# Three gate tiles in place of two behind attention, squares of the attention's result on two engines, LayerNorm begun in the gate tiles

## The chip, the cores and the metric

The kernel runs on one core of a Trainium2 chip. The metric is the device time of one execution in microseconds; the median of three executions of the kernel before is 1280.73 us (1280.35 to 1281.03). A profile is one execution of its own, and its time stands beside the median below. The engines are named as the profile names them: PE multiplies matrices (PEld loads its weights), ACT is ScalarE, DVE is VectorE, POOL is GpSimd, SP issues the DMA transfers.

## The reference

One layer of a streaming encoder: 1024 frames of a new stream and 32 frames of a running one with 512 frames behind it, width 1024, 16 heads of 64. In the reference's terms, with all 1056 frames written as one x:

```
h  = rmsnorm(x)
q, k, v, logf, ga, ua, ub, gb, ma, mb = columns of h @ w_in          # each 1024 wide, logf 16
u  = ua * sigmoid(ub);   conv = causal depthwise conv of u, width 31
o  = softmax(q k' + C[t] - C[s]) v,  C = cumsum(log f), causal, q and k rms-normed per head
ya = (o * silu(ga)) @ w_pa
yb = (silu(layernorm(conv)) * silu(gb)) @ w_pb
m  = sigmoid(ma) * ya + sigmoid(mb) * yb
y  = x + m @ w_out
```

Keys, values, forget gates and the last rows of u are outputs too.

## The kernel before

**Tiles.** Everything is computed transposed: channels on the 128 partitions, the 1056 frames along the free axis. A projection makes 128 output channels at a time, from 8 tiles of input channels ("kt") and 3 chunks of 352 frames. Each number is a sum of two fp16 halves, so that one product is three matmuls: high weight by high input, low by high, high by low (line 199). Three matmuls of one kt and one chunk are a *beat*; an output tile has 24 beats.

**Weights.** Two tiles of weights (512 KB each) are prepared together, as a `Batch`. SP loads them (L111, L180); ACT squares each with the sum along a row (L119, output `junk`, a buffer that nothing reads); POOL casts the two sums (L125); PE totals them over the partitions with a matmul (L132, tile `tot`); DVE makes from that a power of two for the scale (L173, L174, tile `sc`); ACT makes the high halves (L154, `wh`) and DVE the low ones in three pieces (L157, `wl`). The scale of a pair serves both tiles. The batch of the *next* pair is prepared beside the matmuls of this one: the squares 3 and 13 beats after the first tile of the pair begins, the total at its 25th beat, the high halves 29 and 39 beats behind the start, the low ones behind those.

**Order.** PE, ACT, DVE and SP run a written order: `later(n, fn)` puts a piece of work n beats behind the present one, `beat()` issues what has become due, and each engine takes its instructions in the order so issued. An engine that waits holds up all that stands behind it. POOL's order is left to a scheduler. In the last stage (the output projection) SP is free too.

**Stages.** Input projections, convolution, q, k and v, the gate ga (to about 600 us); attention (about 600 to 987 us); a stretch between attention and projections (to about 1012 us) with what is left of the gate tiles; the projection pa (`outproj("pa")`, 192 beats) with LayerNorm beside it; the projection pb; the output projection.

**Attention** runs over 128 units: 8 pairs of heads, 8 blocks of 128 queries, 2 heads. A unit has its products of queries and keys (L1259 to 1261, `psS`), the maximum (DVE, L1268), the exponentials on ACT (L1274, L1289), then the high and low halves PH, transposed by DMA (L1306, tile PT), then, per group of four units and LAG = 8 units later, the products with the values (L1327, `po`). The 24 tiles of the gates gb, ma and mb (`fills`) are the filler: NFILL of them are issued in beats between the units, as many per unit as the number `each` allows, and 36 beats of them behind the last unit, around the last groups of value matmuls. The result goes to DRAM (`s_o`, L1344).

**Between attention and projections.** NFILL = 22, so two gate tiles are left (`last_gate`, 48 beats). Beside them run:

- `a_load`: eight loads of the attention's result, 512 KB each, into tiles `wide` (L1555), at tick 0
- `a_square`: a copy of the 32 sample columns by DVE (L1558) and the square with its row sum on ACT (L1537), at ticks 5 + 3f; the squares' own output goes to `ah`, to be overwritten later
- `norm_a.total` at tick 30: PE's `ptot` (L1542), then DVE's scale `nsc` (L1543, L173, L174)
- `norm_a.halves` at ticks 31 + 2f: high half `ah` on ACT (L1548), low half `al` on DVE (L1549)

**LayerNorm**, per tile f of 128 channels, at 16 beats from one tile to the next: `ln_load` (the convolution's result and the gate gb), `ln_centre` (DVE, L1571 and L1572, from the mean and rstd computed earlier), `ln_swish` (ACT, a Silu of each, L1576 and L1577), `ln_gate` (DVE, L1581), `ln_square` (ACT, L1537). Tile f is centred 2 + 16f beats behind the start of pa. When all are squared, `norm_c.total` (a second `ptot`) and `norm_c.halves` (`c_h`, `c_l`) follow, and then pb can begin.

pa's tiles are evacuated by DVE (L1672) with the gate ma, through a Tanh on ACT (L1639, tile `sma`), which wants another table than the Silu. For each change of table ACT loads one (`ACT_TABLE_LOAD`).

Of the kernel before, what the change touches and what calls it, by code (L numbers as in the profile page):

```python
# [10 lines left out]
BF16 = mybir.dt.bfloat16  # L11
F16 = mybir.dt.float16
I32 = mybir.dt.int32
AF = mybir.ActivationFunctionType
ALU = mybir.AluOpType
# [5 lines left out]
TT = T + TS  # L21
# [3 lines left out]
KT = 8  # L25
# [6 lines left out]
LNEXP = "natural_log_exp_and_others"  # L32
NFILL = 22
R_U, R_V, R_QK, R_G, R_A = 0.21, 0.18, 0.165, 0.23, 0.7
# [23 lines left out]
def build(tc, xT, xt, wv, wf, ckT, cv, clT, stT, vec, cst, yT, kT, vO, lfO, cpT, csT):  # L58
# [33 lines left out]
    class Batch:  # L92


        def __init__(self, keys):
            self.keys = keys
            self.n = len(keys)
            self.raws = []
# [110 lines left out]
    def later(n, fn):  # L209

        pace["n"] += 1
        late.append((pace["tick"] + n, pace["n"], fn))
        late.sort(key=lambda e: e[:2])
# [1204 lines left out]
    K = range(len(units))  # L1418
    each = (BEAT * (24 * NFILL - 36) + sum(map(matmuls, K))) / sum(map(heavy, K))
    events = {}  # L1420
# [101 lines left out]
    class Norm:  # L1522


        def __init__(self, g, junk):
            self.g, self.junk, self.x = g, junk, {}
            self.n8 = cp.tile([128, 8], F32, name="n8", tag="n8", bufs=2)
            self.sc = cp.tile([128, 4], F32, name="nsc", tag="nsc", bufs=2)
            self.back = self.sc[:, 3:4]
            sides["back_" + g] = self.back  # L1530
# [4 lines left out]

        def square(self, f):
            nc.scalar.activation(self.junk()[:, f, :].bitcast(BF16), self.x[f], AF.Square, accum_out=self.n8[:, f:f + 1])  # L1537

# [12 lines left out]

    norm_a = Norm("pa", lambda: ah)

# [3 lines left out]
    def a_square(f):  # L1557
        nc.vector.tensor_copy(norm_a.x[f][:, T:], os_t[:, f, :])  # L1558
        norm_a.square(f)

# [18 lines left out]
    def ln_gate(f):  # L1579
        y = norm_c.x[f]  # L1580
        nc.vector.tensor_mul(y, y, lng.pop(f))  # L1581

    def ln_square(f):
        if not chl:
            chl.extend(cpl.tile([128, KT, TT], F16, name=a, tag=a) for a in ("c_h", "c_l"))
        norm_c.square(f)

# [3 lines left out]

    norm_c = Norm("pb", lambda: chl[0])
    n_gate = 24 * len(fills)
    n_pa, n_pb = n_gate, n_gate + 192
    for f in range(8):
        a_load(f)
        later(5 + 3 * f, lambda f=f: a_square(f))
        later(31 + 2 * f, lambda f=f: norm_a.halves(f, ah, al))
        t = n_pa + 16 * f
        for n, fn in ((-16, ln_load), (2, ln_centre), (8, ln_swish), (13, ln_gate), (16, ln_square)):  # L1600
            later(t + n, lambda f=f, fn=fn: fn(f))
        later(n_pa + 136 + 5 * f, lambda f=f: norm_c.halves(f, *chl))
        t = n_pa + 24 * f
        later(t - 18, lambda f=f: pa_load(f))
        later(t + 1, lambda f=f: pa_gate(f))
        t = n_pb + 24 * f
        later(t - 12, lambda f=PBO[f]: pb_load(f))
        later(t + 1, lambda f=PBO[f]: pb_gate(f))
    later(30, norm_a.total)
    later(n_pa + 134, norm_c.total)  # L1610
    for j in range(3):
# [8 lines left out]
    w_next = []  # L1620
    later(n_pb + 150, lambda: w_next.append(load_raw(("out", 0))))
    later(n_pb + 176, lambda: w_next.append(split_w(w_next.pop(0))))
    sma, ya, mixed = {}, {}, {}

# [21 lines left out]
    cpl = pool("cpl", 1, stack=pcl)  # L1646
    yap = pool("yap", 2, stack=pcl)

    def outproj(g, rh, rl, mk, order=range(8)):
# [83 lines left out]
    order = ExitStack()  # L1733
    order.enter_context(tc.manual_schedule(engines={E.PE, E.DVE, E.Activation}))

# [105 lines left out]
    firsts = [w_next.pop()]  # L1841
    raws = [load_raw(("out", 2))]
    both = [big("r0")]
# [117 lines left out]
```

## Time and profile before

| | before |
|---|---|
| median of three executions | 1280.73 us |
| the profiled execution | 1278.86 us |
| its span | 1277.1 us |
| granted TensorE clock, mean over the span | 0.988 |
| PE busy | 1230.6 us, 96% |
| DVE busy | 1022.4 us, 80% |
| ACT busy | 779.2 us, 61% |
| POOL busy | 556.0 us, 44% |
| tick 0 of the stretch between (its first gate matmul behind the last value matmul) | about 987 us |
| PE's first wait for a total of squares | 1005.20 us |

The span is what the profiler recorded of the program on the engines; the execution's time has a little around it. Idle time of an engine counts only where the engine that ends last waits for it. In the rows that follow, a line number is one of the kernel before; "out<-in" are the names of the tiles; a number in square brackets is the wait ahead of the instruction, with the engine, the tile and the line that ended it.

### The profile page before, as it was taken

How to read it: one execution, taken by the hardware profiler on the slowest of the kernel's cores; microseconds unless marked ns; L12 is line 12 of the kernel's file. 1: busy time of each engine (PE TensorE's matmuls, PEld its weight loads, DVE VectorE, ACT ScalarE, POOL GpSimd, SP SyncE). 2: the span in 40 equal slices, each digit the busy share in tenths (PEclk: the TensorE clock that was granted, in tenths of full speed). 3: DMA queues.
4: the chain of work that ended last, by engine and by line, in shares of the span. 5: the costliest groups of instructions: out<-in, count | busy, mean ns of one | idle time of the engine just before them, and what ended most of it. 6: DMA issues, size and time to landing. Idle time of an engine off the chain costs nothing.

```text
span 1277.1 us, 24881 instructions
## 1 busy us (share of the span) xinstructions
PE 1230.6 (96%) x9288; PEld 856.9 (67%) x9288; DVE 1022.4 (80%) x1453; ACT 779.2 (61%) x1480; POOL 556.0 (44%) x541
## 2 busy tenths in 40 slices
PE   8999999999999999999898998989989899999998
PEld 5677786666666666666665565666657556666898
DVE  5799898888988989798998998976873477577764
ACT  5645655768677684456776666667764878444410
POOL 4058483728566561013554655534442000122662
PEclk8999999999999999999999999999989999999999
DMA  6335251433324247445999999999987876543561
GB/s 233 102 109 148 60 146 43 114 91 111 115 78 123 73 133 224 132 133 154 208 212 227 209 211 214 212 209 213 222 191 185 303 270 206 203 152 119 158 184 63
DMA packets 259802, 207.38 MB, mean 162 GB/s; under 512 B 186464, under 2 KB 222176, under 8 KB 259680
## 3 DMA queue, kind: packets, MB, share of 16 engines
q1 hardware_dynamic: 259536, 205.71, 60.2%
q8 instruction: 73, 1.20, 0.4%
q14 instruction: 49, 0.40, 0.1%
q10 hardware_dynamic: 144, 0.07, 0.0%
HBM read 110.84 MB, written 57.12 MB: 132 GB/s over the span
## 4 chain that ended last, share of the span: by engine, by line
PE 72%; DVE 10%; ACT 5%; issue 5%; DMA 4%; POOL 3%; SPq 0%; DVEq 0%; POOLq 0%; ACTq 0%
PE pj L199 50%; PE pjv L830 7%; PE pj L1791 6%; PE po L1327 2%; DMA PT<-PH 2%; PE psS L1259 2%; PE psS L1260 2%; DVE y L392 1%; DVE nm L1268 1%; POOL PH L1296 1%; DVE wl L157 1%; DVE PH L1298 1%; POOL P L1295 1%; DMA wide<-s_o 1%; ACT PH L1289 1%
## 5 line engine op out<-in xcount | busy, mean ns | idle before, releaser
L199 PEld LDWEIGHTS <-wh 128*128 128x128 f16 x3840 | 377.5, 98 | 207.2 <-issue 6.2
L199 PE MATMUL pj<-xh,wh 128*128 128x352 f16 (+2 forms) x1536 | 482.9, 314 | 0.6 <-DVE qn L976 0.5
L199 PE MATMUL pj<-xl,wh 128*128 128x352 f16 (+2 forms) x1536 | 482.0, 314 | 1.3 <-DVE xl L614 1.3
L199 PE MATMUL pj<-xh,wl 128*128 128x352 f16 (+2 forms) x1536 | 482.2, 314 | 0.1
L392 DVE SCALAR_TENSOR_TENSOR y<-u,vec_t,y 128x1086 f32<-128x1086 f32 x240 | 354.2, 1477 | 4.0 <-ACT y L389 0.9
L199 PEld LDWEIGHTS <-wl 128*128 128x128 f16 x1920 | 188.6, 98 | 89.6 <-issue 1.0
L157 DVE SCALAR_TENSOR_TENSOR wl<-raw,sc,wh 128x384 f16<-128x384 f32 (+1 forms) x236 | 170.1, 743 | 40.8 <-ACT wh L154 39.9
L1274 ACT ACTIVATE P<-psS,nm 128x1024 f32<-128x1024 f32 (+7 forms) x128 | 94.4, 738 | 99.6 <-DVE nm L1268 38.9
L1295 POOL TENSOR_SCALAR P<-P,nm 128x896 f32<-128x896 f32 (+3 forms) x64 | 63.8, 996 | 190.3 <-ACT PH L1289 184.4
L1268 DVE TENSOR_REDUCE nm<-psS 128x1 f32<-128x1024 f32 (+7 forms) x128 | 96.2, 752 | 47.6 <-PE psS L1261 32.4
L1289 ACT ACTIVATE PH<-P,nm 128x1024 f16<-128x1024 f32 (+7 forms) x128 | 98.6, 770 | 9.7 <-DMA PT<-PH 7.7
L1296 POOL TENSOR_TENSOR PH<-P,PH 128x896 f16<-128x896 f32 (+3 forms) x64 | 95.1, 1486 | 5.0
L119 ACT ACTIVATE junk<-raw 128x1024 bf16<-128x1024 f32 x78 | 81.7, 1048 | 5.2 <-DMA raw<-wf 5.1
L961 POOL TENSOR_TENSOR sql<-sqf,sqh 128x352 fp32r<-128x352 f32 x48 | 55.8, 1165 | 65.0 <-ACT sqh L958 64.8
L1259 PE MATMUL psS<-KB,QB 128*128 128x512 f16 (+2 forms) x192 | 64.4, 336 | 19.4 <-ACT P L1274 19.1
L125 POOL CAST topb<-tops 128x2 bf16<-128x2 f32 x32 | 14.8, 462 | 151.8 <-ACT junk L119 151.6
L1298 DVE SCALAR_TENSOR_TENSOR PH<-P,nm,PH 128x896 f16<-128x896 f32 (+3 forms) x64 | 61.7, 964 | 12.7 <-ACT PH L1289 11.5
L154 ACT ACTIVATE wh<-raw,sc 128x1024 f16<-128x1024 f32 (+1 forms) x58 | 64.9, 1124 | 11.0 <-DVE sc L174 11.0
L830 PE MATMUL pjv<-vwh,xh 128*128 128x260 f16 x256 | 70.1, 274 | 0.0
L830 PE MATMUL pjv<-vwl,xh 128*128 128x260 f16 x256 | 70.0, 273 | 0.0
L830 PE MATMUL pjv<-vwh,xl 128*128 128x260 f16 x256 | 69.9, 273 | 0.0
L987 POOL TENSOR_TENSOR ql<-qn,qh 128x352 f16<-128x352 f32 (+1 forms) x48 | 65.7, 1385 | 7.2 <-ACT qh L986 7.1
(309 smaller groups left out, 2377.3 us busy)
## 6 DMA issues: line engine op xcount, KB each, us to landing
raw<-wf SPq DMA_DIRECT2D x92, 512.0 KB
kT<-kun SPq DMA_DIRECT2D x8, 528.0 KB
s_ga<-t SPq DMA_DIRECT2D x24, 176.0 KB
s_gb<-t SPq DMA_DIRECT2D x24, 176.0 KB
s_ma<-t SPq DMA_DIRECT2D x24, 176.0 KB
s_mb<-t SPq DMA_DIRECT2D x24, 176.0 KB
sma<-s_ma SPq DMA_DIRECT2D x8, 528.0 KB
wide<-s_y SPq DMA_DIRECT2D x8, 528.0 KB
```

Of the source, the lines that this page charges most:

```text
L119: nc.scalar.activation(junk[:, :raw.shape[1] * raw.shape[2]], raw.rearrange("p a b -> p (a b)"), AF.Square, accum_out=self.tops[:, i:i + 1])
L157: nc.vector.scalar_tensor_tensor(wl[:, ks, :], raw[:, ks, :], self.s[:, i:i + 1], wh[:, ks, :], op0=ALU.mult, op1=ALU.subtract)
L199: nc.tensor.matmul(ps, a[:, kt, :], b(kt, sl), start=(first and n == 0), stop=(last and n == N - 1))
L392: t = nc.vector.scalar_tensor_tensor(y, u[:, i:i + CW], w, y, op0=ALU.mult, op1=ALU.add)
L830: nc.tensor.matmul(ps[:, :VC], a, b, start=(n == 0), stop=(n == 23))
L1259: nc.tensor.matmul(ps[:, ksl], QB[:, qsl], KB[:, ksl], start=True, stop=False)
L1268: nc.vector.tensor_reduce(self.nm[:, e:e + 1], self.ps[:, :self.w], axis=AX.X, op=ALU.max, negate=True)
L1274: nc.scalar.activation(self.P[:, :self.w], self.ps[:, :self.w], AF.Exp, bias=self.nm[:, e:e + 1], accum_out=self.nm[:, 2 + e:3 + e])
L1289: nc.scalar.mul(self.H[:, :n, 0, :], self.P3, self.f)
L1295: nc.gpsimd.tensor_scalar(self.P3, self.P3, f, 1.0, op0=ALU.mult, op1=ALU.mult)
L1296: nc.gpsimd.tensor_sub(self.H[:, :n, 1, :], self.P3, self.H[:, :n, 0, :])
L1791: nc.tensor.matmul(pss[c][:, :HC], a[:, k, :], x, start=(not more and kt == 0 and n == 0), stop=(kt == 3 and n == 2), skip_group_check=more)
```

## The change

NFILL goes from 22 to 21, so that three gate tiles (72 beats) stand between attention and pa. `each` is now made for 24 x 21 - 18 = 486 beats in the units in place of 24 x 22 - 36 = 492, so that 18 beats of the fillers stay behind the last unit, where there were 36.

The squares of the attention's result go to ACT for even tiles and to DVE for odd ones (a multiplication with its sum). The total moves from tick 30 to 32, the halves from 31 + 2f to 33 + 3f. A table with Silu is asked for at tick 38.

LayerNorm's tiles are counted from the end of attention in place of the start of pa, at 18 beats from one tile to the next: tile f is centred at tick 48 + 18f. In the kernel before, pa began at tick 48, so that it was 50 + 16f. Its loads go out 18 beats ahead of the mark in place of 16. The square's unread output goes to the gate's buffer `g3` and no longer to `c_h`, so that `c_h` and `c_l` are made later. LayerNorm's total stands 121 beats behind the start of pa in place of 134, its halves begin at 124 and are 6 beats apart.

The load of the third weight tile of the output projection is issued at beat 156 of pb, in place of the beginning of the output stage, and in the output stage SP, too, runs in the written order.

```diff
-NFILL = 22
+NFILL = 21
...
-    each = (BEAT * (24 * NFILL - 36) + sum(map(matmuls, K))) / sum(map(heavy, K))
+    each = (BEAT * (24 * NFILL - 18) + sum(map(matmuls, K))) / sum(map(heavy, K))
...
-        def square(self, f):
-            nc.scalar.activation(self.junk()[:, f, :].bitcast(BF16), self.x[f], AF.Square, accum_out=self.n8[:, f:f + 1])
+        def square(self, f, junk, act=True):
+            acc, x = self.n8[:, f:f + 1], self.x[f]
+            if act:
+                nc.scalar.activation(junk, x, AF.Square, accum_out=acc)
+            else:
+                nc.vector.scalar_tensor_tensor(junk, x, 1.0, x, op0=ALU.mult, op1=ALU.mult, accum_out=acc)
...
     def a_square(f):
         nc.vector.tensor_copy(norm_a.x[f][:, T:], os_t[:, f, :])
-        norm_a.square(f)
+        norm_a.square(f, ah[:, f, :].bitcast(BF16), f % 2 == 0)
...
     def ln_gate(f):
         y = norm_c.x[f]
-        nc.vector.tensor_mul(y, y, lng.pop(f))
+        nc.vector.tensor_mul(y, y, lng[f])

     def ln_square(f):
-        if not chl:
-            chl.extend(cpl.tile([128, KT, TT], F16, name=a, tag=a) for a in ("c_h", "c_l"))
-        norm_c.square(f)
+        norm_c.square(f, lng.pop(f).bitcast(BF16)[:, :TT])
...
-        later(31 + 2 * f, lambda f=f: norm_a.halves(f, ah, al))
-        t = n_pa + 16 * f
-        for n, fn in ((-16, ln_load), (2, ln_centre), (8, ln_swish), (13, ln_gate), (16, ln_square)):
+        later(33 + 3 * f, lambda f=f: norm_a.halves(f, ah, al))
+        t = 46 + 18 * f
+        for n, fn in ((-18, ln_load), (2, ln_centre), (8, ln_swish), (13, ln_gate), (16, ln_square)):
             later(t + n, lambda f=f, fn=fn: fn(f))
-        later(n_pa + 136 + 5 * f, lambda f=f: norm_c.halves(f, *chl))
+        later(n_pa + 124 + 6 * f, lambda f=f: norm_c.halves(f, *chl))
...
-    later(30, norm_a.total)
-    later(n_pa + 134, norm_c.total)
+    later(32, norm_a.total)
+    later(38, lambda: nc.scalar.preload_act_table_set("silu_and_others"))
+    later(n_pa + 121, norm_c.total)
...
+    later(n_pb + 156, lambda: raws_out.append(load_raw(("out", 2))))
...
-    order.enter_context(tc.manual_schedule(engines={E.PE, E.DVE, E.Activation}))
+    order.enter_context(tc.manual_schedule(engines={E.PE, E.SP, E.DVE, E.Activation}))
```

What this does to the order of the engines, at two places. A row is line, operation, output and inputs, size; numbers behind a name tell tiles of one name apart.

**DVE behind the total of squares**, before. `ptot` is the total, `nsc` its scale; `al` are the low halves; `sc` is the scale of pa's first two weight tiles, `wl` their low halves; `wide_13047` is LayerNorm's tile 0.

```order
L173 TENSOR_SCALAR sc_12904<-tot_13004 128x2
L174 TENSOR_SCALAR sc_12904<-sc_12904 128x2
L157 SCALAR_TENSOR_TENSOR wl_13023<-raw_12644,sc_12904,wh_13022 128x384
...
L1549 SCALAR_TENSOR_TENSOR al_12867<-wide_12888,nsc_12873,ah_12866 128x1056
L157 SCALAR_TENSOR_TENSOR wl_13084<-raw_12791,sc_12904,wh_13083 128x256
L1549 SCALAR_TENSOR_TENSOR al_12867<-wide_12890,nsc_12873,ah_12866 128x1056
L1571 TENSOR_TENSOR wide_13047<-wide_13047,mean_79 128x1056
L1572 TENSOR_TENSOR wide_13047<-wide_13047,rstd_80 128x1056
L1581 TENSOR_TENSOR wide_13047<-wide_13047,g3_13046 128x1056
```

The same place in the change; `wide_12927` is now LayerNorm's tile 0, `sc_12920` the scale of pa's first two weight tiles. The fifth to eighth tile of the result, `wide_12786` to `wide_12792`, stand among LayerNorm's.

```order
L1553 SCALAR_TENSOR_TENSOR al_12769<-wide_12786,nsc_12775,ah_12768 128x1056
L1575 TENSOR_TENSOR wide_12927<-wide_12927,mean_79 128x1056
L1576 TENSOR_TENSOR wide_12927<-wide_12927,rstd_80 128x1056
L1553 SCALAR_TENSOR_TENSOR al_12769<-wide_12788,nsc_12775,ah_12768 128x1056
L173 TENSOR_SCALAR sc_12920<-tot_13035 128x2
L174 TENSOR_SCALAR sc_12920<-sc_12920 128x2
L1553 SCALAR_TENSOR_TENSOR al_12769<-wide_12790,nsc_12775,ah_12768 128x1056
L157 SCALAR_TENSOR_TENSOR wl_13054<-raw_12649,sc_12920,wh_13053 128x384
L1553 SCALAR_TENSOR_TENSOR al_12769<-wide_12792,nsc_12775,ah_12768 128x1056
...
L1585 TENSOR_TENSOR wide_12927<-wide_12927,g3_12926 128x1056
L157 SCALAR_TENSOR_TENSOR wl_13103<-raw_12865,sc_12920,wh_13102 128x384 x2
```

The scale of the weights stood ahead of the total of squares and stands now behind the sixth low half and the centring of LayerNorm's first tile, which stood behind all eight.

**ACT from the last halves to the squares of pa's second pair of weights**, before. `wh` are pa's first two tiles; `sma` is the gate ma; `raw_12961` and `raw_13092` are the second pair.

```order
L1548 ACTIVATE ah_12866<-wide_12890,nsc_12873 128x1056
L1051 ACTIVATE t_13134<-pj_13097,sc_12522 128x352
L1639 ACT_TABLE_LOAD
L1639 ACTIVATE sma_13029<-sma_13029 128x1056
L119 ACTIVATE junk_13163,tops_13160<-raw_12961 128x1024
L1576 ACT_TABLE_LOAD
L1576 ACTIVATE wide_13047<-wide_13047,vec_t_110 128x1056
L1577 ACTIVATE g3_13046<-g3_13046 128x1056
L119 ACTIVATE junk_13199,tops_13160<-raw_13092 128x1024
```

In the change (`raw_12986` and `raw_13109` are the second pair):

```order
L1552 ACTIVATE ah_12768<-wide_12790,nsc_12775 128x1056
L154 ACTIVATE wh_13053<-raw_12649,sc_12920 128x1024
L1580 ACTIVATE wide_12927<-wide_12927,vec_t_110 128x1056
...
L1539 ACTIVATE g3_12926,n8_12776<-wide_12927 128x1056
L154 ACTIVATE wh_13102<-raw_12865,sc_12920 128x1024
...
L1580 ACTIVATE wide_13015<-wide_13015,vec_t_110 128x1056
L1581 ACTIVATE g3_13014<-g3_13014 128x1056
...
L119 ACTIVATE junk_13178,tops_13175<-raw_12986 128x1024
L1539 ACTIVATE g3_13014,n8_12776<-wide_13015 128x1056
L119 ACTIVATE junk_13220,tops_13175<-raw_13109 128x1024
```

The squares of the second pair, on which PE's next `tot` rests, stood behind the first tile's Silu of LayerNorm and stand now behind its first tile and the second tile's Silu; the last of them also behind the second tile's square, and so behind that tile's gate product on DVE.

More of the change, by code (lines that the diff above doesn't have):

```diff
@@ L1522, in build, with __init__ @@
     class Norm:
-        def __init__(self, g, junk):
-            self.g, self.junk, self.x = g, junk, {}
+        def __init__(self, g):
+            self.g, self.x = g, {}
             self.n8 = cp.tile([128, 8], F32, name="n8", tag="n8", bufs=2)
@@ L1550, in halves @@
                                            op0=ALU.mult, op1=ALU.subtract)
-    norm_a = Norm("pa", lambda: ah)
+    norm_a = Norm("pa")
     def a_load(f):
@@ L1590, in last_gate @@
             pass
-    norm_c = Norm("pb", lambda: chl[0])
+    norm_c = Norm("pb")
     n_gate = 24 * len(fills)
@@ L1621, in build @@
     later(n_pb + 150, lambda: w_next.append(load_raw(("out", 0))))
+    later(n_pb + 156, lambda: raws_out.append(load_raw(("out", 2))))
     later(n_pb + 176, lambda: w_next.append(split_w(w_next.pop(0))))
+    raws_out = []
     sma, ya, mixed = {}, {}, {}
@@ L1647, in build @@
     yap = pool("yap", 2, stack=pcl)
+    chl.extend(cpl.tile([128, KT, TT], F16, name=a, tag=a) for a in ("c_h", "c_l"))
     def outproj(g, rh, rl, mk, order=range(8)):
@@ L1841, in build @@
     firsts = [w_next.pop()]
-    raws = [load_raw(("out", 2))]
+    raws = raws_out
     both = [big("r0")]
```

## The prediction

> **What bounds the kernel now.** The page's first lines come first.
>
> ```profile
> span 1277.1 us, 24881 instructions
> PE 1230.6 (96%) x9288; PEld 856.9 (67%) x9288; DVE 1022.4 (80%) x1453; ACT 779.2 (61%) x1480; POOL 556.0 (44%) x541
> ```
>
> PE is busy 96% of the span, and the change neither adds nor removes a projection, so it can only move the few places where PE stands still or runs at a lower clock. Next the view of windows by stage: six windows of attention (600 to 960 us) with their sum, then the gate tiles behind attention, then LayerNorm beside the pa projections.
>
> ```profile
> core 0: us, PE busy (x) PEld busy (x) DVE busy (x) ACT busy (x) POOL busy (x), PEclk, DMA share, GB/s
> ...
> sum 360.00, PE 333.35 PEld 221.32 DVE 301.77 ACT 240.50 POOL 184.49; mean PE 55.56 PEld 36.89 DVE 50.30 ACT 40.08 POOL 30.75
> 987.00:1011.80 24.80, 20.52 (x139) 13.26 (x137) 4.53 (x10) 17.11 (x28) 0.64 (x3) 1.00 0.90 327
> 1011.80:1100.00 88.20, 85.21 (x564) 55.20 (x563) 70.73 (x97) 70.63 (x83) 4.21 (x9) 0.98 0.68 235
> ```
>
> PE idles 26.65 us (7%) in attention, 4.28 behind it, 2.99 in the LayerNorm stage. The timeline of PE behind attention gives the places; in brackets stand the wait and who ended it. These are all the waits of 0.4 us or more there.
>
> ```profile
> 999.25 0.16 PE L132 MATMUL tot<-topb,ones_b 128*128 128x2 bf16 x1 [0.74 <-POOL topb L125]
> 1005.20 0.39 PE L1542 MATMUL ptot<-n,ones_f 128*128 128x8 f32 x2 [3.54 <-ACT ah L1537]
> 1027.03 0.16 PE L132 MATMUL tot<-topb,ones_b 128*128 128x2 bf16 x1 [2.17 <-POOL topb L125]
> 1078.53 0.39 PE L1542 MATMUL ptot<-n,ones_f 128*128 128x8 f32 x2 [0.81 <-ACT c_h L1537]
> 1197.25 0.39 PE L1791 MATMUL pj<-mh,wl 128*128 128x264 f32 x1 [0.41 <-POOL wl L1743]
> ```
>
> The first four sum to 7.26 us: two are the total of the squares of the attention's result and of LayerNorm's, two the maxima of a pair of weight tiles. What a wait does to the granted clock is in the windows right behind them (the clock is the third number from the end).
>
> ```profile
> 1005.20:1008.80 3.60, 3.60 (x25) 2.46 (x26) 1.20 (x5) 2.40 (x3) 0.46 (x2) 1.00 0.97 298
> 1027.00:1033.00 6.00, 5.97 (x30) 3.50 (x30) 5.15 (x8) 4.71 (x6) 0.27 (x1) 0.72 0.27 95
> 943.34 0.59 PE L1259 MATMUL psS<-KB,QB 128*128 128x512 f16 x1 [3.53 <-ACT P L1274]
> 943.34:946.80 3.46, 3.46 (x20) 1.77 (x20) 1.75 (x3) 2.02 (x6) 0.00 (x0) 0.50 0.92 221
> 946.80:955.00 8.20, 8.20 (x52) 4.99 (x50) 6.26 (x14) 5.12 (x12) 1.50 (x2) 0.87 0.70 157
> ```
>
> After the 3.54 us the clock stays at 1.00; after the 2.17 it is 0.72 for 6 us (6 x 0.28 = 1.7 us lost); after 3.53 in attention it is 0.50, then 0.87 (3.46 x 0.50 + 8.2 x 0.13 = 2.8). So the stage between attention and pb loses 7.26 + 1.7 = **8.9 us**, which is what the change can win.
>
> **The order of the queues.** One beat is three matmuls; the chain of waits gives its length.
>
> ```profile
> 1116.11 21.50 PE pj L199 x144
> 988.36 4.76 SPq L1555 DMA_DIRECT2D wide<-s_o  x8
> 992.46 9.65 DMA wide<-s_o
> ```
>
> 48 beats in 21.50 us: 0.448 a beat, 0.149 a matmul. The eight loads of the attention's result go out from 988.36 and the last lands at 992.46 + 9.65 = 1002.11, 13.75 us later.
>
> *The total of squares.* Call X the end of the last value matmul, where the third gate tile now begins. The loads start about 1.1 us behind X (store, then issue, as now), so the last lands at X + 14.9 by the row; two weight loads that shared this time are gone from it, say X + 14. The last square is now DVE's. The nearest price is DVE's multiply-and-sum elsewhere in the kernel:
>
> ```profile
> L551 DVE SCALAR_TENSOR_TENSOR sq<-xtok 128x1024 f32<-128x1024 f32 x2 | 2.4, 1216 | 0.0
> ```
>
> 1.3 us for 1056 columns makes X + 15.5 with a copy ahead of it. PE asks at tick 32, X + 14.3. The wait of 3.54 becomes **1.2** (0 to 3: earlier landing, or DVE's accumulation twice as dear). The first weight maximum (0.74) is asked for at tick 49 now, 17 beats or 7.6 behind the total; ACT is done with its squares at 4.2 in the walk below, so it goes to 0.
>
> *Halves and LayerNorm.* They now share ACT and DVE from this point. Durations:
>
> ```profile
> 1008.47 0.54 ACT L1051 ACTIVATE t<-pj,sc 128x352 f32<-128x352 f32 x1
> 1008.90 3.30 ACT L1548 ACTIVATE ah<-wide,nsc 128x1056 f16<-128x1056 f32 x3
> 1012.10 1.14 ACT L154 ACTIVATE wh<-raw,sc 128x1024 f16<-128x1024 f32 x1
> 1018.40 1.28 ACT L1639 ACT_TABLE_LOAD   x1
> 1019.70 1.08 ACT L1639 ACTIVATE sma<-sma 128x1056 f32<-128x1056 f32 x1
> 1023.40 1.27 ACT L1576 ACTIVATE wide<-wide,vec_t 128x1056 f32<-128x1056 f32 x1 [0.28 <-DVE wide L1572]
> 1024.57 1.07 ACT L1577 ACTIVATE g<-g 128x1056 f32<-128x1056 f32 x1
> 1025.55 1.04 ACT L119 ACTIVATE junk<-raw 128x1024 bf16<-128x1024 f32 x1
> 1026.96 1.08 ACT L1537 ACTIVATE c_h<-wide 128x1056 bf16<-128x1056 f32 x1 [0.29 <-DVE wide L1581]
> 1009.83 0.61 DVE L157 SCALAR_TENSOR_TENSOR wl<-raw,sc,wh 128x384 f16<-128x384 f32 x1
> 1011.99 3.77 DVE L1549 SCALAR_TENSOR_TENSOR al<-wide,nsc,ah 128x1056 f16<-128x1056 f32 x3
> 1020.82 1.25 DVE L1571 TENSOR_TENSOR wide<-wide,mean 128x1056 f32<-128x1056 f32 x1
> 1025.67 1.26 DVE L1581 TENSOR_TENSOR wide<-wide,g 128x1056 f32<-128x1056 f32 x1 [2.31 <-ACT g L1577]
> ```
>
> Operations of one engine overlap by about 0.1 (24.57 to 25.55 is 0.98 for a duration of 1.07), so from start to start I take ah 1.08, t 0.44, wh 1.04, table 1.30, first Silu 1.17, gate's Silu and sma 0.98, junk 1.04, a square on ACT 1.07; on DVE al 1.25, a tile's centring 2.4, the gate product 1.2, wl 0.53. I walk the two queues by the order shown ahead, from time 0 at the total of squares; its result is there for ACT at 1.0.
>
> - ACT does six halves, the weight square, the table and two evictions by 10.7 (ah5 ends at 10.3), ah6 at 11.8. DVE follows: al2 7.9, al3 9.4, al4 10.7, tile 0 centred 13.1, al5 14.3, and only then the scale of pa's first two weight tiles, 14.7.
> - ACT's next is wh of pa0: it stands idle **2.9** us (11.8 to 14.7). wh 15.7, Silu 16.9, gate's Silu 17.9, ah7 19.0, an eviction 19.4.
> - DVE waits for ah7, then al7 20.3, two pieces of wl 21.2, gate product 22.4. ACT's square of tile 0 waits for that: **3.0** idle. Square 23.5, wh of pa1 24.6, eviction 25.0.
> - DVE: wl 25.7, tile 1 centred 28.1; ACT's Silu waits for it, **3.1** idle. Silu 29.3, gate 30.3, eviction and sma 31.7, weight square of pa2 32.7, LayerNorm's square 33.8, weight square of pa3 34.9, POOL's cast 35.3.
>
> PE reaches the maximum of pa2/pa3 at tick 97, 65 beats behind tick 32: 65 x 0.448 = 29.1. It waits 35.3 - 29.1 = **6.2 us**, in the place of the 2.17. Bounds: 0, if those three idles (9.0 in all) mostly don't happen; about 7 if each is some tenths longer. In the old order ACT met no such idles, because the weights' scale stood ahead of the halves on DVE and LayerNorm behind them all. pa0 itself is safe: needed at 40 beats, 17.9, with wh at 15.7 and the first wl at 16.4.
>
> *The clock* behind a wait of 6.2: the rows give 1.7 and 2.8, I take 2.2 (0 to 2.8). [...]
>
> *LayerNorm's total* (0.81): its last square comes 14 beats ahead of the total as against 6; I take 0.4 (0 to 0.8).
>
> Stage after: 1.2 + 6.2 + 2.2 + 0.4 = 10.0 against 8.9: **+1.1**.
>
> **Attention.** 72 projection matmuls leave it: 30 from between the last two groups of value matmuls, 24 from behind the last, and 18 (6 beats, 2.7 us) from its units, 0.02 us a unit.
>
> ```profile
> PE psS L1259 <- ACT P L1274: 19.1, 15, 3.5
> 976.19 6.82 PE pj L199 x45
> 983.01 0.61 PE po L1327 x12
> 975.22 1.19 SPq L1306 DMA_TRANSPOSE PT<-PH  x1
> 607.70 6.29 SPq L1306 DMA_TRANSPOSE PT<-PH  x2
> 616.37 0.27 PE L1327 MATMUL po<-PT,Vh 128*64 128x256 f16 x1 [1.25 <-DMA PT<-PH]
> ```
>
> Moved matmuls are free where PE is the limit, and cost their 2.7 us where they filled a wait that stays. PE waited 7% of attention, 19.1 us of it for ACT's exponentials: I take 0.5 (0 to 2.7). At the tail the last value matmuls had 6.82 us of cover behind the ones before; now 15 matmuls, 2.2 us, so they are asked for at 976.2 + 2.2 = 978.4. The transposition they need was issued until 976.41; an earlier one that was issued until 613.99 released PE at 616.37, 2.4 us behind, which here would be 978.8. So 0.2 (0 to 0.4). The squares on DVE fall in the window behind attention, in which it is busy 4.53 of 24.80 us, and two high halves of gate tiles that ACT makes there in POOL's place (2 x 1.1) precede its squares and the loads' landing; the freed junk buffer and the table loaded once fewer (1.28) lie inside the walk. The output stage idles 0.41 before its first matmuls; a fixed order of SP's loads there changes an engine with transfers in hand long before their use: 0 (0 to 1.3).
>
> **Sum:** 1.1 + 0.5 + 0.2 = +1.8 on the profiled execution's 1278.86: 1280.7. The median lies 1280.73 - 1278.86 = 1.87 above that execution, so **1282.5 us**.
>
> **Rivals.** *A, ACT keeps up: faster.* Its own work in the walk, from 1.0 to the end of pa3's square, is 8 halves, 3 weight squares, 2 wh, 2 tiles of LayerNorm with their squares, 5 evictions, sma and a table: 8.6 + 3.1 + 2.1 + 6.4 + 2.2 + 1.0 + 1.3 = 24.8; with cast 26.2, which fits into 29.1. If the idles sum to under 2.9, no total is missed and no clock lost: the stage costs 1.2 + 0.4 = 1.6, 7.3 less; with attention's 0.7, 1282.5 - 8.4 = 1274.1. For it: the walk has ±2 us in it, and ACT and DVE already alternate in the old order with a wait of 2.31 for the gate product. Against: the order on DVE is fixed, and the scale stands behind al5. *B, attention is paced by its own chain: slower.* If exponentials and not PE set the units' pace, all 2.7 us taken out turn into waits, and one of them lengthens enough to drop the clock (1.7; in the rows somewhere between 0.8 and 2.2 us of wait it begins). Then 2.7 + 1.7 in the place of 0.5: 1286.4. For it: 19.1 us of waits for one operation, up to 3.53 each. Against: 93% busy, so most units wait for nothing. *C, nothing is begun earlier.* Counted from the end of attention, LayerNorm's tile f is centred at tick 48 + 18f as against 50 + 16f before: from f = 1 on it isn't earlier at all, only pa is 24 beats later. If the tot wait stays near 2 with its 1.7, and the total of squares near 2.5, the stage is 6.6 and the sum -1.6: 1279.1.
>
> **How the numbers follow.** About 0.2% (2.56 us) is what a measurement can tell from no change. Forecast 0.43 (1282.5, its own range 1279.5 to 1285.5: 0.31 same, 0.12 slower); A 0.25 (0.23 faster, 0.02 same); B 0.2 (0.18 slower, 0.02 same); C 0.12 (0.07 same, 0.03 faster, 0.02 slower). Faster 0.26, same 0.42, slower 0.32. The range leaves out half of A's spread downwards and the upper third of B's: 1274.5 to 1287.5, some 0.8 of the whole. All bounds at once (stage 0 to 13.6, attention 0 to 3.1, output 0 to 1.3) would reach from 1271.8 to 1289.8.
>
> **What would show it.** Right: one wait of 5 to 7 us ahead of the weight maximum behind 25 beats of pa's first tile, a clock of 0.5 to 0.8 behind it; ACT idle about 3 us ahead of pa0's wh, waiting for DVE's scale; the total of squares waited for 0 to 3 us; attention's windows of 60 us busy as before. Wrong: that wait under 2 us (A, or C if the squares' total still costs 2 or more), or waits in attention's units that grow by over 2 us (B).

## The result: slower by 0.9%, and where it went

The changed kernel takes 1292.12 us (median of four, 1290.34 to 1292.71), the kernel before 1280.54 beside it: a ratio of 1.0089, 95% interval 1.0072 to 1.0107. The forecast was 1282.5 with a range up to 1287.5. The profiled execution's span went from 1277.1 to 1290.5.

The changed kernel's waits of PE of 0.4 us or more behind attention (start, duration, in brackets the wait and who ended it):

```profile
991.50 0.36 PE L1546 MATMUL ptot<-n,ones_f 128*128 128x8 f32 x2 [2.67 <-ACT junk L119]
1027.20 0.16 PE L132 MATMUL tot<-topb,ones_b 128*128 128x2 bf16 x1 [4.54 <-POOL topb L125]
1197.62 0.39 PE L1797 MATMUL pj<-mh,wl 128*128 128x264 f32 x1 [0.40 <-POOL wl L1749]
1210.44 0.39 PE L1797 MATMUL pj<-mh,wh 128*128 128x264 f32 x1 [0.68 <-ACT wh L1745]
1211.52 0.39 PE L1797 MATMUL pj<-mh,wl 128*128 128x264 f32 x1 [0.68 <-POOL wl L1749]
1217.90 0.39 PE L1797 MATMUL pj<-tf,wh 128*128 128x264 f32 x1 [0.41 <-ACT wh L1745]
1219.35 0.39 PE L1797 MATMUL pj<-tf,wl 128*128 128x264 f32 x1 [1.06 <-POOL wl L1749]
1234.37 0.52 PE L1797 MATMUL pj<-mh,wh 128*128 128x264 f32 x1 [2.79 <-DVE r L1834]
1254.72 0.39 PE L1797 MATMUL pj<-tf,wh 128*128 128x264 f32 x1 [0.58 <-DVE r L1809]
1270.90 0.39 PE L1797 MATMUL pj<-tf,wh 128*128 128x264 f32 x1 [0.57 <-DVE r L1809]
```

Of the five waits of before, the first two and the two at 1027 and 1078 have become two, in sum 7.21 us as against 7.26. What is new stands behind 1197, in the output stage (L1797): eight waits, 7.17 us, where there was one of 0.41.

To split the span by stage I take the first and the last start of four groups of matmuls: the products of queries and keys (psS), the value products (po), pa and pb (their low halves al and c_l). Before:

```profile
L1259 PE MATMUL psS<-KB,QB x192: 216/376/634, 581.9 to 966.6; 128*128 128x512 f16 x96, 128*128 128x384 f16 x32, 128*128 128x128 f16 x32, 128*128 128x256 f16 x32
L1327 PE MATMUL po<-PT,Vh x640: 219/273/422, 614.8 to 983.4; 128*64 128x256 f16 x128, 128*64 128x128 f16 x32
L199 PE MATMUL pj<-c_l,wh x192: 311/312/313, 1105.0 to 1190.6; 128*128 128x352 f16 x192
```

After:

```profile
L1259 PE MATMUL psS<-KB,QB x192: 216/376/417, 579.6 to 961.9; 128*128 128x512 f16 x96, 128*128 128x384 f16 x32, 128*128 128x128 f16 x32, 128*128 128x256 f16 x32
L1327 PE MATMUL po<-PT,Vh x640: 218/273/417, 612.5 to 974.2; 128*64 128x256 f16 x128, 128*64 128x128 f16 x32
L199 PE MATMUL pj<-c_l,wh x192: 311/313/313, 1105.4 to 1191.0; 128*128 128x352 f16 x192
```

| stretch | before, us | after, us | difference | predicted |
|---|---|---|---|---|
| start to the first psS | 581.9 | 579.6 | -2.3 | 0 |
| first psS to the last po | 401.5 | 394.6 | +0.3 | +0.7 |
| last po to the first of pb | 121.6 | 131.2 | +2.4 | +1.1 |
| pb | 85.6 | 85.6 | 0 | 0 |
| output stage to the end of the span | 86.5 | 99.5 | **+13.0** | 0 (bound 1.3) |

For the second and third row 48 matmuls (7.2 us) that changed sides of the last po are counted back. The -2.3 at the start is no effect of the change: nothing was edited there, and the window from 20 to 40 us had a granted clock of 0.83 in the profile of before and 1.00 in that of after.

```profile
20.00:40.00 20.00, 18.95 (x114) 13.21 (x113) 13.60 (x31) 12.56 (x25) 3.00 (x4) 0.83 0.08 29
20.00:40.00 20.00, 18.41 (x129) 12.79 (x126) 15.70 (x42) 13.07 (x26) 2.93 (x4) 1.00 0.07 26
```

(The first row is before, the second after; the third number from the end is the clock.) So the part on which the prediction spent nearly all its words came out near its sum (by terms that partly differ, see below), and the line that it dismissed in half a sentence, SP's written order in the output stage, is the result.

**What SP does there.** Its timeline in the changed kernel; the time of a row is from the first issue to the end of the last, waits inside it included. yT are stores of finished pieces, raw the loads of output weights, r the loads of the residual.

```profile
1208.37 0.88 SPq L180 DMA_DIRECT2D raw<-wf  x2
1209.35 14.49 SPq L1810 DMA_DIRECT2D yT<-r  x4
1223.89 1.40 SPq L1814 DMA_DIRECT2D r<-xT  x3
1225.39 0.85 SPq L180 DMA_DIRECT2D raw<-wf  x2
```

The two loads at 1225.39 are those of the second pair of output weights, by their place in SP's order. Before, the loads of the same pair went out at

```profile
1206.87 0.37 SPq L180 DMA_DIRECT2D raw<-wf  x1
...
1207.96 0.34 SPq L180 DMA_DIRECT2D raw<-wf  x1
```

In the changed kernel the four stores from 1209.35 on hold SP for 14.49 us, since each waits for DVE's last addition to its piece, and the loads that stand behind them go out some 18 us later than they did. It is neither the first hold nor the longest: at the first store SP waited 33.5 us, until 1205.15. Behind that store stood the load of the last of the four tiles that come ahead of the pairs (1205.60; before 1184.46) and the two loads of the first pair (from 1208.37; before 1190.94 and 1200.82). The views of waits say what comes of the holds. Of SP before, then of SP, DVE and ACT after (us in total, times, longest), all from 1190 us on:

```profile
SPq L1804 <- DVE r L1803: 34.7, 21, 7.2
```

```profile
SPq L1810 <- DVE r L1809: 92.6, 20, 33.5
DVE sa L1768 <- DMA raw<-wf: 21.0, 4, 8.3
ACT wh L1745 <- DMA raw<-wf: 7.9, 1, 7.9
```

SP's waits at stores go from 34.7 to 92.6 us, and DVE, which waited for no weight load before, waits 21.0 us for four. While it does, the additions that empty PE's accumulators stand behind it, and PE's 2.79 at 1234.37 is named after one of them ("DVE r"):

```profile
1233.28 0.69 DVE L1768 TENSOR_TENSOR sa<-raw 128x512 f32<-128x512 f32 x1 [4.65 <-DMA raw<-wf]
1233.89 0.42 DVE L1834 TENSOR_TENSOR r<-u,pj 128x264 f32<-128x264 f32 x1
```

The chain of waits now holds a load of some 7 us for each of the last three pairs (7.33, 7.09 and 7.04).

Of the 13.0 us, 6.8 are waits of PE as listed (7.17 - 0.41) and 3.4 are the clock (3.4 x 0.50 + 3.5 x 0.49), in one window behind the waits at 1217.90 and 1219.35 and one behind that at 1234.37; the rest I can't place in single rows.

```profile
1220.80:1224.20 3.40, 3.40 (x15) 3.40 (x16) 2.22 (x4) 1.00 (x3) 3.40 (x4) 0.50 0.00 0
1234.40:1237.90 3.50, 3.50 (x16) 3.50 (x17) 3.40 (x5) 1.05 (x1) 1.75 (x2) 0.51 0.11 39
```

### The profile page after: what moved, and what is told of

Read it like the earlier page. It is cut to its first block, busy times and chain, and to the rows that moved or that the text cites. A ratio compares the mean times of both kernels' runs of the same rounds, so it can differ in the third digit from the quotient of the medians.

```text
span 1290.5 us, 24883 instructions
## 1 busy us (share of the span) xinstructions
PE 1233.1 (96%) x9288; PEld 858.2 (67%) x9288; DVE 1025.9 (79%) x1461; ACT 776.3 (60%) x1473; POOL 551.2 (43%) x539
## 4 chain that ended last, share of the span: by engine, by line
PE 66%; DVE 13%; DMA 6%; issue 6%; ACT 5%; POOL 3%; SPq 1%; DVEq 0%; ACTq 0%; POOLq 0%
PE pj L199 50%; PE pjv L830 7%; DVE nm L1268 2%; DVE wl L157 2%; DMA PT<-PH 2%; DMA raw<-wf 2%; DVE y L392 2%; PE po L1327 2%; POOL wl L1749 2%; DVE PH L1298 2%; PE pj L1797 1%; PE psS L1259 1%; PE psS L1260 1%; ACT PH L1289 1%; ACT P L1274 1%
## 5 line engine op out<-in xcount | busy, mean ns | idle before, releaser
L157 DVE SCALAR_TENSOR_TENSOR wl<-raw,sc,wh 128x384 f16<-128x384 f32 (+1 forms) x236 | 166.4, 728 | 39.4 <-ACT wh L154 39.2
L1296 POOL TENSOR_TENSOR PH<-P,PH 128x896 f16<-128x896 f32 (+3 forms) x64 | 89.7, 1402 | 4.9
L1259 PE MATMUL psS<-KB,QB 128*128 128x512 f16 (+2 forms) x192 | 62.9, 327 | 25.3 <-ACT P L1274 25.3
```

Of the source, the lines that this page charges most:

```text
L157: nc.vector.scalar_tensor_tensor(wl[:, ks, :], raw[:, ks, :], self.s[:, i:i + 1], wh[:, ks, :], op0=ALU.mult, op1=ALU.subtract)
L1259: nc.tensor.matmul(ps[:, ksl], QB[:, qsl], KB[:, ksl], start=True, stop=False)
L1296: nc.gpsimd.tensor_sub(self.H[:, :n, 1, :], self.P3, self.H[:, :n, 0, :])
```

## The experiments

The times of one kernel spread by some 4 us to either side with the clock that it is granted (one kernel below ran in 1278.82 at a mean clock of 0.993 and in 1285.22 at 0.988), so ratios with their intervals are compared; kernels of one group ran on one chip with the kernel before among them.

### SP's order: undone, alone, and with the stores out of the way

*SP free again in the output stage, all else as changed:*

```diff
-    order.enter_context(tc.manual_schedule(engines={E.PE, E.SP, E.DVE, E.Activation}))
+    order.enter_context(tc.manual_schedule(engines={E.PE, E.DVE, E.Activation}))
```

> The change with one edit undone: SP is free again in the output stage. In the traces the output stage takes 86.2 us before (1190.9 to the end) and 99.2 us after the change (1191.3 to the end); all else together 2.7 us less 2.3 us of a faster start. Theory 1 (SP's written order delays the loads of the output weights behind stores that wait): the 13 us come back, 1292.1 - 13 = 1279 by the profiles, 1283 if the start of the profiled execution was lucky; 1278 to 1285. Theory 2 (the third output weight tile, loaded earlier, takes a buffer or bandwidth from what stands behind it, and SP's order is harmless): stays at 1289 to 1293.

Measured: 1281.68 us, ratio 1.0015 (0.9998 to 1.0032).

*The kernel before with SP's written order in the output stage and nothing else* (the same line the other way round):

> The kernel before with this one edit alone: SP in the written order in the output stage. Theory 1: the 13 us appear here without anything else, 1280.5 + 13 = 1293.5 (1291 to 1297; a little more is possible, since the third weight tile is loaded late here). Theory 2: 1280 to 1281.5, as before.

Measured: 1291.04 us, ratio 1.0081 (1.0057 to 1.0104). One word in one line makes nearly the whole difference between the two kernels.

*The change with SP in the written order, each store written 24 beats later:*

```diff
-                nc.sync.dma_start(yT[f, :, hf * HT + sl.start:hf * HT + sl.stop], x[:, sl])
+                later(24, lambda: nc.sync.dma_start(yT[f, :, hf * HT + sl.start:hf * HT + sl.stop], x[:, sl]))
```

> The change, SP still in the written order, but each store of a finished piece is written 24 beats (about 9 us) later, behind the next loads of weights. Theory 1 in its strict form (a store that waits for DVE holds the loads behind it): most of the 13 us come back, 1280 to 1284. If it is instead the loads' own written place (17 beats, 6.2 us, ahead of their use, with 7.3 us from issue to landing) and not the stores: 1288 to 1292, because the place of the loads among the beats is unchanged. Theory 2: 1289 to 1293.

Measured: 1280.51 us, ratio 1.0004 (0.9990 to 1.0017). The loads keep their place among the beats, and yet all of it comes back, so it isn't the written order as such, nor the loads' place, but the waiting store ahead of the load. SP's timeline of this kernel:

```profile
1209.82 1.53 SPq L180 DMA_DIRECT2D raw<-wf  x2
1211.45 5.68 SPq L1810 DMA_DIRECT2D yT<-r  x4
1217.18 1.42 SPq L1814 DMA_DIRECT2D r<-xT  x3
1218.65 0.90 SPq L180 DMA_DIRECT2D raw<-wf  x2
```

The second pair's loads go out at 1209.82 and the third's at 1218.65, ahead of the stores that hold SP. Behind the last start of pb's matmuls (1191.6) the span of 1278.1 has 86.5 us, as before.

*The change without both its edits in the output stage* (SP free, the third weight tile loaded at the beginning of the stage):

```diff
-    later(n_pb + 156, lambda: raws_out.append(load_raw(("out", 2))))
...
-    raws = raws_out
+    raws = [load_raw(("out", 2))]
```

> The change without both of its edits in the output stage (SP free, the third weight tile loaded at the stage's beginning as before): what is left is attention, gate tiles, squares and LayerNorm. The prediction's sum for these was +1.8 us: 1282.3, bounds as there (1274 to 1287). The two profiles, stage by stage, give +0.4 in attention and +2.3 from the gate tiles to the end of pb: 1283.2. Theory 1 has it within 1 us of the kernel with only SP undone; theory 2 has it lower than that one by most of 13.

Measured: 1286.03 us, ratio 1.0040 (1.0025 to 1.0054). That is 4.4 above the kernel that differs from it in this load alone, where theory 1 had the two within 1 us, while its profiled execution, 1280.44, was the lowest of its ten and shows no wait in the output stage but one of 0.40. I tried the pair again further down, on a better base.

### The weight maximum: why ACT is late

From here on the base is the kernel with late stores. *Only the centring of LayerNorm's tiles on DVE 3 beats later,* behind the scale of pa's first weights:

```diff
-        for n, fn in ((-18, ln_load), (2, ln_centre), (8, ln_swish), (13, ln_gate), (16, ln_square)):
+        for n, fn in ((-18, ln_load), (5, ln_centre), (8, ln_swish), (13, ln_gate), (16, ln_square)):
```

> The kernel with the stores written late, and in it only the centring of LayerNorm's tiles on DVE moved 3 beats later, so that the scale of pa's first two weight tiles stands ahead of it; ACT's order is unchanged. Base: 1280.5 us, total of squares waited for 1.2, weight maximum at tick 97 waited for 6.2. Theory 1 (the scale's place on DVE alone makes ACT late, the first of its three idles): wh of pa0 2.4 us earlier, the rest follows, the wait at tick 97 falls to 3 to 4 and the time to about 1277. Theory 2 (ACT and DVE alternate in lock step through the first two LayerNorm tiles, and a gain at one step is lost at the next): the wait stays at 5 to 7, the time within 1.5 us of 1280.5.

Measured: 1279.87 us, ratio 1.0015 (1.0003 to 1.0028), as against the base's 1.0004: no gain. PE's waits at the total of squares and at the weight maximum in its profile (two more, of 0.44 and 1.00, stand at 1071.27 and 1072.43, the second at LayerNorm's total):

```profile
991.12 0.36 PE L1546 MATMUL ptot<-n,ones_f 128*128 128x8 f32 x2 [2.50 <-ACT junk L119]
1026.17 0.16 PE L132 MATMUL tot<-topb,ones_b 128*128 128x2 bf16 x1 [3.88 <-POOL topb L125]
```

The wait of 3.88 looks like theory 1, but it is shorter mostly because PE was slower on its way there. Behind its wait of 2.50 at the total, the clock was 0.58 for 4 us, which is 1.7 us lost (4 x 0.42); the base has 1.00 in the same place, by a window shown in the last section.

```profile
991.10:995.10 4.00, 3.98 (x17) 2.24 (x18) 2.28 (x5) 3.39 (x4) 0.19 (x1) 0.58 0.94 292
```

What ACT and DVE set is the distance from the total to the maximum: 1026.17 - 991.12 = 35.05 here, and in the base 1028.67 - 992.97 = 35.70:

```profile
992.97 0.36 PE L1546 MATMUL ptot<-n,ones_f 128*128 128x8 f32 x2 [1.17 <-DVE ah L1541]
1028.67 0.16 PE L132 MATMUL tot<-topb,ones_b 128*128 128x2 bf16 x1 [6.21 <-POOL topb L125]
```

0.65 us gained of the 2.4 that the first step should have given: theory 2.

*LayerNorm 6 beats later and 17 apart:*

```diff
-        t = 46 + 18 * f
+        t = 52 + 17 * f
...
-        later(n_pa + 124 + 6 * f, lambda f=f: norm_c.halves(f, *chl))
+        later(n_pa + 126 + 6 * f, lambda f=f: norm_c.halves(f, *chl))
...
-    later(n_pa + 121, norm_c.total)
+    later(n_pa + 124, norm_c.total)
```

> The kernel with the stores written late, and LayerNorm's tiles begun 6 beats later (2.7 us), 17 beats apart in place of 18, its total 3 beats later. In the order of ACT, all halves and wh of pa1 then stand ahead of the first LayerNorm square, and of LayerNorm's second tile nothing waits ahead of the first weight square of the next pair. Theory 2 expects no wait for DVE ahead of those squares worth more than 1 us, the wait at tick 97 at 0 to 1 in the place of 6.2, and the clock's loss behind it (2 to 3 us) gone: 1280.5 - 5.5 - 2.5 = 1272.5 (1270 to 1275). The rival (these waits don't lie on the path that sets the end, because attention or LayerNorm's total takes them up): a wait of 3 or more at LayerNorm's total, time 1278 to 1281.

Measured: 1273.89 us, ratio 0.9960 (0.9943 to 0.9977). From the last po to the output stage the only waits of PE over 0.15 us in its profile are 0.47 for a transposition at 975.76 and

```profile
992.85 0.53 PE L1546 MATMUL ptot<-n,ones_f 128*128 128x8 f32 x2 [2.00 <-DVE ah L1541]
```

The wait at the weight maximum is gone, and none came in its place at LayerNorm's total. Begun *later*, LayerNorm costs less.

*The same, and the total of the attention's squares at tick 36, its halves with it:*

```diff
-        later(33 + 3 * f, lambda f=f: norm_a.halves(f, ah, al))
+        later(37 + 3 * f, lambda f=f: norm_a.halves(f, ah, al))
...
-    later(32, norm_a.total)
+    later(36, norm_a.total)
```

> As the kernel with LayerNorm 6 beats later, and besides the total of the attention's squares 4 beats later (36 in place of 32), the halves with it. Where the total's wait is 1.2 to 3.5 us (the runs so far), 4 beats are 1.8 us of it; the chain of ACT and DVE behind the total isn't touched in time, so PE reaches tick 97 that much earlier. Theory 2: wait at the total 0 to 1.5, at tick 97 0 to 1.5, time 0 to 2 us under the kernel without this step. The rival (the chain behind the total sets the end): the wait saved at the total comes back at tick 97, equal times.

Measured: 1271.81 us, ratio 0.9941 (0.9918 to 0.9964). In the profile the total's wait is 0.73 and the maximum's none. By the two ratios the step is worth 0.2%; their intervals overlap, so its size isn't settled.

*The kernel before, with two gate tiles and all squares on ACT, and only LayerNorm later:*

```diff
-        t = n_pa + 16 * f
+        t = n_pa + 10 + 16 * f
...
-        later(n_pa + 136 + 5 * f, lambda f=f: norm_c.halves(f, *chl))
+        later(n_pa + 144 + 5 * f, lambda f=f: norm_c.halves(f, *chl))
...
-    later(n_pa + 134, norm_c.total)
+    later(n_pa + 142, norm_c.total)
```

> The kernel before with two gate tiles and all squares on ACT, and only LayerNorm 10 beats later, its total and halves 8 later. If the order of LayerNorm among ACT's other work is what costs, this must help without a third gate tile: the wait of 2.2 at the weight maximum and its clock loss of 1.7 go, the total of squares still costs 3.5, LayerNorm's total grows from 0.8 to some 2.3: 1280 - 2.4 = 1277.5 (1275.5 to 1280). If the third gate tile is needed for the gain, it stays at 1279.5 to 1282.

Measured: 1275.54 us, ratio 0.9983 (0.9968 to 0.9999). The wait at the maximum goes here too, LayerNorm's total, expected at some 2.3, is not waited for, and the total of squares keeps its 3.54, where the four kernels with a third tile and the total at 36 have 0.73 to 2.55:

```profile
1003.37 0.40 PE L1542 MATMUL ptot<-n,ones_f 128*128 128x8 f32 x2 [3.54 <-ACT ah L1537]
```

With LayerNorm out of the way, the kernel with the third tile and the total at 36 is at 0.9941 and this one at 0.9983, and the intervals don't touch; those of the two kernels with SP free further down (0.9954 and 0.9966) overlap with it. So what the third tile is worth is not settled, and whether two tiles with a later total would do as well was not tried.

### Squares on one engine, and the third weight tile again

*The fastest so far, with all squares on ACT:*

```diff
-        norm_a.square(f, ah[:, f, :].bitcast(BF16), f % 2 == 0)
+        norm_a.square(f, ah[:, f, :].bitcast(BF16), True)
```

> The fastest kernel so far (stores late, LayerNorm 6 beats later, total at 36; 0.7 us of wait at the total), with all eight squares of the attention's result on ACT again. Theory 1 (the loads of the result, one in 1 to 1.5 us, set the end of the squares, and one engine at 1.07 us a square keeps up): the total's wait and the time stay within 1 us, 1271 to 1273. Theory 2 (the second engine is what shortens the wait of 3.5 us in the kernel before): the last squares queue up on ACT by 1 to 3 us, the total is waited for 2 to 4, and the time is 1273 to 1276.

Measured: 1269.93 us, ratio 0.9937 (0.9916 to 0.9958): the second engine is worth nothing that can be seen here. Beside 0.66 at the maximum, PE waits for

```profile
992.50 0.39 PE L1546 MATMUL ptot<-n,ones_f 128*128 128x8 f32 x2 [1.21 <-ACT ah L1539]
```

*The fastest with SP free and the stores in their old place* (the third weight tile early), and *the same with that tile loaded at the beginning of the stage*:

> The fastest kernel so far with SP free in the output stage and the stores where the change has them; the third output weight tile is loaded early, as in the change. Two ways to free the loads from the waiting stores should be equal: within 1.5 us of 1271.8. If the written order with late stores is itself worth something: 1273 to 1275.

> As the one with SP free, and the third output weight tile loaded at the output stage's beginning, as before. Of the two kernels that differed in this alone, the late one was 4.4 us slower by its median (1286.0 and 1281.7), while their profiles had the output stage at 86.5 and 86.4. Theory 1 (the place of this load is worth nothing; the 4.4 us were another draw of the clock): equal times within 1.5 us. Theory 2 (the late load delays the first products): 3 to 5 us slower than its neighbour, with a wait of PE or a lower clock at the beginning of the output stage.

Measured: 1271.24 us, ratio 0.9954 (0.9936 to 0.9972), and 1273.05 us, ratio 0.9966 (0.9953 to 0.9980). SP free or with late stores is equal within the intervals. The late load costs 1.8 us by the medians, the ratios overlap, and both profiles have a single wait in the output stage, of 0.38 and 0.37. So the 4.4 of the first pair did not come back at their size: what made them, and whether this load is worth 0, 1 or 2 us, stays open.

The two kernels with the lowest ratios: LayerNorm later, total at 36, stores late, with squares on one engine or two (0.9937 and 0.9941, that is about 0.6% under the kernel before).

## Why the prediction was wrong, step by step

- **SP's order in the output stage: 0 (0 to 1.3) predicted, +13.0 in the profile, +0.8% when done alone.** This is the step that failed. It argued that "a fixed order of SP's loads there changes an engine with transfers in hand long before their use". In the kernel before those loads were early *because* SP was free: they had been put ahead of the stores that were written before them. The prediction shows no row of SP from the output stage, and in the order of the changed kernel stores stand ahead of every pair of loads. And the bound had no row behind it that speaks of a waiting store, though one stood in the view of waits: SP waited 34.7 us at stores even when it could choose.
- **The walk of ACT and DVE: right.** Predicted idles of ACT 2.9 ahead of wh of pa0, 3.0 ahead of the first LayerNorm square, 3.1 ahead of the second Silu. The timeline of ACT:

```profile
1006.32 1.15 ACT L154 ACTIVATE wh<-raw,sc 128x1024 f16<-128x1024 f32 x1 [2.94 <-DVE sc L174]
...
1014.21 1.08 ACT L1539 ACTIVATE g<-wide 128x1056 bf16<-128x1056 f32 x1 [3.10 <-DVE wide L1585]
...
1020.11 1.27 ACT L1580 ACTIVATE wide<-wide,vec_t 128x1056 f32<-128x1056 f32 x1 [3.24 <-DVE wide L1576]
```

  From total to maximum the walk gave 35.3, and it was 35.70. The cause that the text leaned on, the scale behind the centring, was only the first of the three steps: taken away alone it gained 0.65 us. It is the alternation over LayerNorm's first two tiles.
- **The wait at the maximum: 6.2 predicted, 4.54 measured, 6.21 in the kernel with late stores.** It is what is left of the 35.7 when PE arrives, and PE arrived later because it had lost 1.7 us of clock behind the total (windows below): 4.54 + 1.7 = 6.2. In the kernel with late stores it lost none there.
- **The total of squares: 1.2 (0 to 3) predicted, 2.67 measured,** and from 1.17 to 3.96 in the other five kernels with the total at 32. The mechanism was right (the last square began at 990.08, after 1.23 us of waiting for its load, its sum ended at 991.34, and PE began at 991.50); the size varies from run to run by more than the bound, and the second engine isn't what sets it. The largest is in the kernel without both edits in the output stage.
- **The clock: 2.2 predicted, for one wait; 4.7 measured, for two.** The windows behind the total and the maximum:

```profile
991.50:994.00 2.50, 2.50 (x12) 1.48 (x13) 0.80 (x4) 1.93 (x3) 0.19 (x1) 0.62 0.87 242
994.00:1000.00 6.00, 6.00 (x37) 3.73 (x36) 3.77 (x4) 5.97 (x8) 0.46 (x1) 0.87 0.64 247
1027.20:1030.00 2.80, 2.80 (x11) 1.49 (x11) 0.93 (x1) 2.80 (x3) 0.00 (x0) 0.50 1.03 413
1030.00:1034.00 4.00, 4.00 (x19) 2.15 (x17) 2.75 (x8) 2.33 (x4) 0.27 (x1) 0.61 0.44 146
```

  2.5 x 0.38 + 6 x 0.13 = 1.7 behind the wait of 2.67, and 2.8 x 0.50 + 4 x 0.39 = 3.0 behind that of 4.54. So the stage lost 2.67 + 4.54 + 4.7 = 11.9, where 10.0 were predicted and 8.9 stood before: 3.0 more, 2.4 by the starts of the matmuls.
- **LayerNorm's total: 0.4 predicted, none over 0.15 measured.**
- **Attention: +0.7 predicted, +0.3 measured, but not for the prediction's reasons.** The 48 matmuls taken out of the stretch left it 6.9 us shorter, of 7.2. Its windows, before and after, show two larger terms behind that:

```profile
581.90:983.40 401.50, 374.85 (x3061) 248.80 (x3060) 327.22 (x501) 268.84 (x596) 198.60 (x165) 0.97 0.94 205
579.60:974.20 394.60, 364.71 (x3015) 242.80 (x3012) 323.22 (x495) 268.93 (x593) 194.55 (x163) 0.99 0.93 206
```

  PE stood still for 26.7 us (401.50 - 374.85) and now for 29.9, and its waits for the exponentials grew from the 19.1 of the prediction's row to

```profile
PE psS L1259 <- ACT P L1274: 25.3, 21, 2.8
```

  That is rival B's own sign, waits that grow by over 2 us. What offset it is a better clock, 0.99 for 0.97. The idling is no accident of one run: from 575 to 960 us PE idles 27.0 to 29.5 us in four kernels with three gate tiles (the change, SP free, late stores, both edits undone), 26.7 and 26.5 in two with two (before, SP's order alone). Its waits for the exponentials in L1259 are 19.4 to 26.1 us in seven kernels with three tiles, 19.1 to 19.8 in three with two. Whether the better clock belongs to the change is not shown.
- **Without the output stage the sum holds in part:** +1.8 us predicted; +1.8 measured with SP free (ratio 1.0015, its interval reaching just below 1), +0.6 with late stores, but +6.1 (ratio 1.0040) with both edits of the output stage undone, the kernel nearest to what the sum was made for. The range of 1274.5 to 1287.5 held all three.
- **Rival A had most of the prize right and the way to it wrong.** It put the stage without the wait at 1274.1, which is 6.6 under the kernel before, and gave it a chance if the walk were 2 us off. The walk wasn't off; but moving LayerNorm 6 beats later does take the wait away, and 4.7 under the kernel before was measured (1273.89 beside 1278.57).
- **Rival C** named a fact that mattered more than its chance: counted from the end of attention, LayerNorm begins hardly earlier; what is harmful is that it stands among the halves.

## What to carry to other kernels

SP, issuing in a written order, waited at a store for its data (33.5 us at the first, 92.6 at 20), and the loads behind it waited too: before fixing such an order, list for each load what stands ahead of it, and write stores far behind the loads that they would hold up. That transfers are early in a profile is no evidence that they stay so when the freedom that made them early is taken away (1206.87 with SP free, 1225.39 without). Where two engines hand tiles to and fro, measure the distance between two fixed points of the chain, not the wait at its end (here 35.05 and 35.70 between them, with waits of 3.88 and 6.21), and try the work that alternates *later* too, not only earlier.

## What was unexpected of the hardware

The same wait had a lower clock behind it in one run and not in the other. The total of squares was waited for 3.54 us in the kernel before, with a clock of 1.00 behind it, and for 3.54 us in the kernel before with LayerNorm later, where the next 3.3 us have 0.53:

```profile
1003.40:1006.70 3.30, 3.30 (x13) 1.83 (x14) 1.00 (x4) 2.10 (x3) 0.46 (x2) 0.53 0.67 192
```

Behind waits of 1.17 and 1.21 us the windows show no loss of clock:

```profile
993.00:997.00 4.00, 4.00 (x28) 2.71 (x29) 2.32 (x5) 3.73 (x6) 0.19 (x1) 1.00 0.92 288
992.50:996.20 3.70, 3.70 (x26) 2.52 (x27) 0.61 (x4) 3.68 (x7) 0.38 (x2) 1.00 0.29 86
```

Two small waits close together had a lower clock behind them: the two of 0.41 and 1.06 at 1217.90 and 1219.35 in the changed kernel have the window of 0.50 behind them that is shown with the result, while a single wait of 1.06 at 1217.91 in the kernel before with SP's written order has 1.00 behind it (1220 to 1224).

So the length of a wait alone doesn't tell what clock comes behind it: 2.67 us had 0.62 behind it in the changed kernel, 0.41 and 1.06 close together had 0.50, and one wait of 3.54 had 1.00. And what filled SP's time at the end of the changed kernel was not issuing (0.34 to 0.47 us an issue from 1205 to 1243) but waiting in order, 92.6 us at stores; no run here moved a transfer to another engine.
